# Four edits to the gated feed-forward stages of a two-layer encoder: other places for tiles, other queues for turns, fewer and later seven-product blocks, additions by DMA

## The chip, the cores and the metric

The kernel runs on one core of a Trainium2 chip, as one program. The metric is the device time in microseconds (us) of one execution; the time before is the median of three timed runs. The profile is that of one further execution, whose own time is given beside its span.

## The reference, cut to what matters

The program computes two layers of an encoder over 256 tokens of width 2048 in float32. Each layer is an attention mixer and then a gated feed-forward stage; only the second is touched.

```python
def conv_ffn(x, w_up, conv_w, conv_b, w_down):          # D_FF = 5632
    h = jnp.einsum("bsd,df->bsf", x, w_up)
    g, u = h[..., :D_FF], h[..., D_FF:]
    gp = jnp.pad(g, ((0, 0), (1, 1), (0, 0)))
    g = conv_w[0] * gp[:, :-2] + conv_w[1] * gp[:, 1:-1] + conv_w[2] * gp[:, 2:] + conv_b
    return jnp.einsum("bsf,fd->bsd", jax.nn.gelu(g) * u, w_down)

def reference(...):
    for layer in range(2):
        ...
        h = h + mix
        h = h + conv_ffn(rmsnorm(h, ln_ffn[layer]), ...)
    return rmsnorm(h, ln_final)
```

In the program `g` is the gate, `u` the factor.

## The kernel before

**Products.** Every float32 matrix is split in two parts that TensorE multiplies in its rounded float32 form: a high part (a cast on ScalarE, line 231) and the rest (a subtraction on VectorE, line 234). A product is then three matmuls, high by high, high by low and low by high (lines 195 to 197). Weights stream from HBM in units of 128 x 1024 values: a load on SyncE's queue into one of five `raw` places, the cast into one of four `wh`, the subtraction into one of four `wl`. A unit holds 256 input rows for 512 columns, and feeds twelve matmuls of 128 x 512 (two token halves, two blocks of 128 rows, three matmuls each).

**The feed-forward stage.** 5632 hidden values are 44 blocks of 128, taken four at a time: `up_group` j makes 512 columns of the gate (`x` = 0) and 512 of the factor (`x` = 1), each for both token halves, in four `gm` banks of PSUM, over eight units. Groups 0 to 5 are the first half, 6 to 10 the second (`HALVES`). After a half's groups its products go through the down projection: `chunk_pair` takes two output chunks of 512 columns at a time, chunks 0 and 1, then 2 and 3, over 12 units in the first half and 10 in the second, and `finish_chunk` adds each chunk's result to the residual `h` (line 376). The last pair of the program is handled by `finish_all`.

**Seven products.** Where two chunks share a unit, the eight block products of a 2 x 2 by 2 x 2 matrix product (24 matmuls) can be made with seven (21 matmuls). This is done for one unit of every `up_group` (`UPK`) and for some units of the down projection: for blocks 1 to 4 of the first half and 1 to 3 of the second, counted from the half's first (in the program's last pair for the first two of them). `column_forms` makes sums and differences of the weights on VectorE (lines 944 to 948) and splits them; `row_forms` does the same for the left operand; `seven_products` (lines 970 to 972) gathers in four extra PSUM banks, `b1`, `b5`, `b6`, `b7`, what belongs to several results. After the last seven-product unit of a pair, `extra_sums` adds them to `h` on VectorE (lines 978 to 989).

**From tokens to features.** At the end of a group each side is scaled from PSUM into a tile (line 877, two instructions, one for each token half), turned in blocks of 32 x 32 on VectorE (line 279) and put in its place by sixteen DMAs of 32 KB each (line 273), eight on SyncE's queue and eight on GpSimd's. Both sides use the same tile, `sc`, so the factor's first instruction waits until the gate's DMAs have read it. `convolved` (lines 893 to 898) then runs on the gate, and `multiplied` (line 921) makes the product, its forms where the block is a seven-product one, and its split parts `prod`.

**What sets the order.** The program is written in order with a small list of things to do later (`later`, `tick`). A scheduler then orders the instructions of each engine, but for those that `keep_in_program_order` pins. Each engine and each queue works strictly in its order. Tiles with one tag share a ring of places; the scheduler adds the waits.

## Time and profile before

| | |
|---|---|
| median of three runs | 2413.26 us (2413.17 to 2413.91) |
| profiled execution, its own time | 2413.16 us |
| its span (first to last instruction) | 2411.4 us |
| TensorE busy | 2392.2 us, 99% |
| VectorE busy | 1881.6 us, 78% |
| ScalarE busy | 1378.7 us, 57% |
| GpSimd busy | 436.4 us, 18% |
| HBM read | 458.48 MB, 191 GB/s over the span |
| feed-forward stages | about 661 to 1372 us and 1690 us to the end |

Matmuls overlap each other, so the mean duration of one (390 ns for 128 x 512) is longer than the time from one to the next, and a busy TensorE says that matmuls follow each other, not at which pace. Idle time of TensorE stands in the waits, with the instruction that ended it. A group's line gives its count, its busy time, the mean of one, and the idle time of its engine just before. "Landing" is the time from a DMA's issue until its data is there. The rows of lines, timelines and waits use the line numbers printed above.

### The profile page before, as it was taken

To read this page: it belongs to the slowest core of one execution; us is meant where nothing else is said; L and a number is where in the kernel's file an instruction comes from. 1 tells how busy PE (TensorE), PEld (TensorE's weight loads), DVE (VectorE), ACT (ScalarE), POOL (GpSimd) and SP (SyncE) were. 2 spreads that over 40 slices of the span, in tenths; PEclk is the share of its full clock that TensorE was granted. 3 is DMA by queue.
4 is the path that set the end of the run, shared out by engine and by line. 5 is a ranking of instruction groups with operands and counts; after the bars stand their busy time and mean duration, and the time that the engine had idled before them with its cause. 6 is when DMAs were issued, how large, how long until landed. Compare 5 with 4: busy or idle time off the path is not lost. (4 is left out here: it accounts for less than half of the span.)

```text
span 2411.4 us, 33193 instructions
## 1 busy us (share of the span) xinstructions
PE 2392.2 (99%) x10883; PEld 1977.5 (82%) x10883; DVE 1881.6 (78%) x2491; ACT 1378.7 (57%) x1960; POOL 436.4 (18%) x764
## 2 busy tenths in 40 slices
PE   9999999999999999999999999999999999999998
PEld 7888888888888888888788888888887888888787
DVE  6576567666778898878889867776788988789897
ACT  6455455566665565545656667555665655555554
POOL 1042033322211211002121200322112210022210
PEclk9999999999999999999999999999999999999999
DMA  8678678766767777667776754667677766677774
GB/s 305 205 196 239 197 195 240 216 201 185 219 193 228 212 221 206 208 204 212 218 213 213 241 185 139 189 198 211 188 228 218 219 197 208 215 213 220 226 214 152
DMA packets 329773, 505.66 MB, mean 210 GB/s; under 512 B 204152, under 2 KB 205560, under 8 KB 329600
## 3 DMA queue, kind: packets, MB, share of 16 engines
q1 hardware_dynamic: 304720, 475.92, 62.8%
q0 software_dynamic: 24448, 26.97, 7.1%
q8 instruction: 85, 1.39, 0.2%
q14 instruction: 88, 0.72, 0.1%
q10 hardware_dynamic: 432, 0.66, 0.1%
HBM read 458.48 MB, written 2.18 MB: 191 GB/s over the span
## 5 line engine op out<-in xcount | busy, mean ns | idle before, releaser
L231 ACT CAST wh<-raw 128x1024 fp32r<-128x1024 f32 (+1 forms) x897 | 931.9, 1048 | 799.4 <-PE gm L197 589.9
L234 DVE TENSOR_TENSOR wl<-raw,wh 128x1024 fp32r<-128x1024 f32 (+1 forms) x897 | 1081.4, 1216 | 380.1 <-ACT wh L231 363.6
L196 PE MATMUL gm<-wl,yT 128*128 128x512 f32 x2092 | 815.8, 390 | 3.1 <-DVE wl L234 2.9
L195 PE MATMUL gm<-wh,yT 128*128 128x512 f32 x2092 | 814.8, 391 | 2.8 <-DVE sc L877 2.8
L197 PE MATMUL gm<-wh,yT 128*128 128x512 f32 x2092 | 812.1, 390 | 0.1
L196 PEld LDWEIGHTS gm<-wl,yT 128*128 128x128 f32 x2092 | 392.8, 188 | 86.7 <-DVE wl L234 6.8
L195 PEld LDWEIGHTS gm<-wh,yT 128*128 128x128 f32 x2092 | 392.7, 188 | 85.6 <-DVE sc L877 4.0
L197 PEld LDWEIGHTS gm<-wh,yT 128*128 128x128 f32 x2092 | 392.7, 188 | 83.0 <-DVE yT L240 0.6
L273 POOL DMA_DIRECT2D qk<-sc x352 | 202.4, 583 | 1047.0 <-DVE sc L279 381.4
L196 PE MATMUL gm<-wl,prod 128*128 128x512 f32 x486 | 189.3, 389 | 0.0
L195 PE MATMUL gm<-wh,prod 128*128 128x512 f32 x486 | 188.7, 389 | 0.0
L197 PE MATMUL gm<-wh,prod 128*128 128x512 f32 x486 | 188.3, 389 | 0.0
L195 PEld LDWEIGHTS gm<-wh,prod 128*128 128x128 f32 x486 | 91.2, 188 | 19.5 <-DVE sc L877 0.4
L196 PEld LDWEIGHTS gm<-wl,prod 128*128 128x128 f32 x486 | 91.2, 188 | 19.2 <-DVE wl L234 0.3
L197 PEld LDWEIGHTS gm<-wh,prod 128*128 128x128 f32 x486 | 91.2, 188 | 19.0
L273 POOL DMA_DIRECT2D qk<-z x128 | 73.9, 585 | 172.5 <-DVE z L279 156.0
L196 PE MATMUL gm<-wl,mix 128*128 128x512 f32 x256 | 100.1, 391 | 0.8 <-DVE wl L234 0.8
L195 PE MATMUL gm<-wh,mix 128*128 128x512 f32 x256 | 100.0, 391 | 0.0
L197 PE MATMUL gm<-wh,mix 128*128 128x512 f32 x256 | 99.6, 390 | 0.0
L273 POOL DMA_DIRECT2D hT<-z x72 | 41.4, 583 | 194.4 <-PE gm L197 75.6
L856 ACT ACTIVATE sum<-sum,rstd 128x512 f32<-128x512 f32 x88 | 60.3, 719 | 12.9 <-DVE sum L847 12.9
L279 DVE STREAM_TRANSPOSE sc<-sc 128x1024 f32<-128x1024 f32 (+1 forms) x55 | 66.7, 1212 | 1.0
(355 smaller groups left out, 2716.0 us busy)
## 6 DMA issues: line engine op xcount, KB each, us to landing
raw<-in_up SPq DMA_DIRECT2D x352, 512.0 KB, 4.6
raw<-in_down SPq DMA_DIRECT2D x176, 512.0 KB, 4.4
raw<-in_eva_qk SPq DMA_DIRECT2D x96, 512.0 KB, 4.4
raw<-in_eva_v SPq DMA_DIRECT2D x46, 512.0 KB, 5.2
raw<-in_evb_qk SPq DMA_DIRECT2D x32, 512.0 KB, 4.8
raw<-in_ev_out SPq DMA_DIRECT2D x32, 512.0 KB, 4.3
raw<-in_od_qk SPq DMA_DIRECT2D x32, 512.0 KB, 4.1
raw<-in_od_out SPq DMA_DIRECT2D x32, 512.0 KB, 4.4
```

What stands on the lines that cost most here:

```text
L195: T.matmul(ps[t], ah, wh[:, sl], start=(kt == 0), stop=False)
L196: T.matmul(ps[t], ah, wl[:, sl], start=False, stop=False)
L197: T.matmul(ps[t], al, wh[:, sl], start=False, stop=(kt == nk - 1))
L231: first = S.copy(dst_h, src)
L234: V.tensor_tensor(dst_l, src, dst_h.bitcast(F32), op=ALU.subtract)
L273: (nc.sync if i % 2 else G).dma_start(dst[j * 32:(j + 1) * 32, :, i * 32:(i + 1) * 32], z[i * 32:(i + 1) * 32].rearrange("p (b j c) -> p b ...
L279: V.transpose(p, p)
L856: S.activation(sums[x][t], sums[x][t], AF.Copy, scale=rstd[0][:, t:t + 1])
```

## The change

- The factor's tile is `z` from another pool, and no longer the gate's `sc`. The second of the two scaling instructions is pinned to its place in the program.
- In these turns three of four source blocks are moved by GpSimd's queue: twelve DMAs there and four on SyncE's, instead of eight and eight. Other turns keep eight and eight.
- The first half has three seven-product blocks (1, 2, 3) instead of four. In each block it is the second of its two units and not the first: units 3, 5, 7 and not 2, 4, 6 (and 8).
- The forms of the left operand have other places, since `z` is taken: the first block's in `rw` and `bias`.
- `extra_sums` makes its two intermediate sums on VectorE and copies `b1` and `b5` on ScalarE; four DMAs of GpSimd that add to their destination, in order, bring them into `h`. In the second half the units that both chunks share before the last ones number 8 instead of 7.

```diff
-HALVES = ((0, 6, (1, 2, 3, 4)), (6, 11, (1, 2, 3)))
+HALVES = ((0, 6, (1, 2, 3)), (6, 11, (1, 2, 3)))
...
-    def moved(z, dst):
+    def moved(z, dst, on_sync=(1, 3)):
...
-                (nc.sync if i % 2 else G).dma_start(
+                (nc.sync if i in on_sync else G).dma_start(
...
-            z = new_sc().rearrange("p t (f k) -> p (t f) k", k=P)
+            z = (tmp.tile([P, 8, P], F32, name=nm("z"), tag="z", bufs=1) if x else
+                 new_sc().rearrange("p t (f k) -> p (t f) k", k=P))
             for t in range(2):
-                V.scalar_tensor_tensor(...)
+                out = V.scalar_tensor_tensor(...)
+                if t:
+                    tc.keep_in_program_order(out)
...
-            turned(z..., sides[x]...)
+            turned(z..., sides[x]..., (3,))
...
-        f = form_sums(*(c4[:, k, t * P:(t + 1) * P] for k in range(2) for t in range(2)))
+        f = form_sums(*(c4[:, 2 + k, t * P:(t + 1) * P] for k in range(2) for t in range(2)))
...
-            forms[2 * (j - g0)] = row_forms(c4, *new_forms(g0, seven.index(j - g0)))
+            forms[2 * (j - g0) + 1] = row_forms(c4, new_forms(g0, seven.index(j - g0)))
...
     def extra_sums(extra, c):
         b1, b5, b6, b7 = extra
-        s = tmp.tile([P, 512], F32, name=nm("sum"), tag="rx")
+        s, x0, s5, x1 = (tmp.tile([P, 512], F32, name=nm("sum"), tag=tag) for tag in ("rx", "ry", "ry", "rx"))
         S.copy(s, b1)
-        V.tensor_tensor(hchunk(0, c), hchunk(0, c), s, op=ALU.add)
-        V.tensor_tensor(s, s, b6, op=ALU.add)
-        V.tensor_tensor(hchunk(0, c + 1), hchunk(0, c + 1), s, op=ALU.add)
-        def rest():
...
-        later(1, rest)
+        S.copy(s5, b5)
+        V.tensor_tensor(x0, s, b6, op=ALU.add)
+        V.tensor_tensor(x1, x0, b7, op=ALU.add)
+        def added(dst, src):
+            tc.keep_in_program_order(G.dma_start(dst, src, accum_op=ALU.add))
+        def twice(x):
+            return x.unsqueeze(1).to_broadcast([P, 2, 512])
+        added(hchunk(0, c), s)
+        added(hchunk(0, c + 1), x0)
+        added(two(h[:, 1, c * 512:(c + 2) * 512]), twice(x1))
+        added(h[:, :, (c + 1) * 512:(c + 2) * 512], twice(s5))
...
-        pss = pair_head(src, c, act, forms, sorted(forms), nu - 3, nk)
+        heads = nu - 3 if nu > 10 else nu - 2
+        pss = pair_head(src, c, act, forms, sorted(forms), heads, nk)
```

How the instructions stand on the engines follows from the scheduler. First place: VectorE at the end of group 0, before the change (`gm` are the group's PSUM banks, `wl` the low parts of weight units, lines 894 and 896 the convolution):

```order
L234 TENSOR_TENSOR wl_6526<-raw_6523,wh_6525 128x1024
L877 SCALAR_TENSOR_TENSOR sc_6462<-gm_6081,rstd_6182,sum_6235 128x4x128
L894 SCALAR_TENSOR_TENSOR qk_6448<-qk_6358,convw,qk_6448 128x255 x2
L896 SCALAR_TENSOR_TENSOR qk_6448<-qk_6358,convw,qk_6448 128x255 x2
L894 SCALAR_TENSOR_TENSOR qk_6448<-qk_6358,convw,qk_6448 128x255 x2
L896 SCALAR_TENSOR_TENSOR qk_6448<-qk_6358,convw,qk_6448 128x255 x2
L877 SCALAR_TENSOR_TENSOR sc_6462<-gm_6082,rstd_6182,sum_6237 128x4x128
L234 TENSOR_TENSOR wl_6544<-raw_6541,wh_6543 128x1024
L279 STREAM_TRANSPOSE sc_6462<-sc_6462 128x1024
```

The same place on VectorE in the changed program (line 878 answers to 877, 897 and 899 to 894 and 896, 952 to 945):

```order
L878 SCALAR_TENSOR_TENSOR z_6462<-gm_6081,rstd_6182,sum_6235 128x4x128
L878 SCALAR_TENSOR_TENSOR z_6462<-gm_6082,rstd_6182,sum_6237 128x4x128
L234 TENSOR_TENSOR wl_6544<-raw_6541,wh_6543 128x1024
L279 STREAM_TRANSPOSE z_6462<-z_6462 128x1024
L952 TENSOR_TENSOR raw_6576<-raw_6577,raw_6576 128x512
L234 TENSOR_TENSOR wl_6584<-raw_6577,wh_6583 128x1024
L897 SCALAR_TENSOR_TENSOR qk_6448<-qk_6358,convw,qk_6448 128x255 x2
L899 SCALAR_TENSOR_TENSOR qk_6448<-qk_6358,convw,qk_6448 128x255 x2
```

The two scaling instructions now follow each other, and the convolution stands behind the turn and behind another weight unit. Second place: VectorE some fifteen instructions on, in group 1, before (line 921 multiplies gate and factor, lines 845 to 848 sum the extra banks of the group's seven-product unit):

```order
L234 TENSOR_TENSOR wl_6634<-raw_6631,wh_6633 128x1024
L921 TENSOR_TENSOR qk_6448<-qk_6448,qk_6465 128x1024
L845 TENSOR_TENSOR sum_6623<-sum_6622,tp_6574 128x512
L234 TENSOR_TENSOR prod_6560<-qk_6448,prod_6560 128x256
L234 TENSOR_TENSOR prod_6563<-qk_6448,prod_6563 128x256
L234 TENSOR_TENSOR prod_6566<-qk_6448,prod_6566 128x256
L234 TENSOR_TENSOR prod_6569<-qk_6448,prod_6569 128x256
L846 TENSOR_TENSOR sum_6624<-sum_6623,s_6575 128x512
L234 TENSOR_TENSOR wl_6652<-raw_6649,wh_6651 128x1024
```

The same place on VectorE in the changed program (line 928 answers to 921):

```order
L234 TENSOR_TENSOR wl_6634<-raw_6631,wh_6633 128x1024
L234 TENSOR_TENSOR wl_6652<-raw_6649,wh_6651 128x1024
L928 TENSOR_TENSOR qk_6448<-qk_6448,qk_6465 128x1024
L845 TENSOR_TENSOR sum_6623<-sum_6622,tp_6574 128x512
L234 TENSOR_TENSOR wl_6674<-raw_6671,wh_6673 128x1024
L234 TENSOR_TENSOR prod_6560<-qk_6448,prod_6560 128x256
L234 TENSOR_TENSOR prod_6563<-qk_6448,prod_6563 128x256
L234 TENSOR_TENSOR prod_6566<-qk_6448,prod_6566 128x256
L234 TENSOR_TENSOR prod_6569<-qk_6448,prod_6569 128x256
L846 TENSOR_TENSOR sum_6624<-sum_6623,s_6575 128x512
L234 TENSOR_TENSOR wl_6692<-raw_6689,wh_6691 128x1024
```

Two weight units that stood behind the run of other work, `wl_6652` and the one after it, now stand ahead of it and in its middle. Third place: VectorE in the second half's first pair of the first layer, in the changed program (lines 987 and 988 are the two sums that are left, line 376 adds a finished chunk to `h`; the first two are chunk 0, the last two chunk 1):

```order
L234 TENSOR_TENSOR wl_11802<-raw_11799,wh_11801 128x1024
L987 TENSOR_TENSOR sum_11726<-sum_11725,tp_11514 128x512
L988 TENSOR_TENSOR sum_11728<-sum_11726,s_11515 128x512
L234 TENSOR_TENSOR wl_11820<-raw_11817,wh_11819 128x1024
L234 TENSOR_TENSOR wl_11867<-raw_11864,wh_11866 128x1024
L376 TENSOR_TENSOR h<-h,gm_11387 128x512
L376 TENSOR_TENSOR h<-h,gm_11388 128x512
L308 STREAM_TRANSPOSE z_11780<-h 128x1024
L234 TENSOR_TENSOR wl_11885<-raw_11882,wh_11884 128x1024
L234 TENSOR_TENSOR wl_11903<-raw_11900,wh_11902 128x1024
L376 TENSOR_TENSOR h<-h,gm_11389 128x512
L376 TENSOR_TENSOR h<-h,gm_11390 128x512
```

Beside it GpSimd's queue at that place, with the semaphores that each DMA waits for (`DMASW` are those of GpSimd's DMAs; the third and fourth carry two chunks each):

```order
L991 DMA h<-sum_11725 128x512 [waits DMASW6_49,Activation_49]
L991 DMA h<-sum_11726 128x512 [waits DMASW7_49,DVE_49]
L991 DMA h<-sum_11728 128x2x512 [waits DMASW0_49,DVE_49]
L991 DMA h<-sum_11727 128x2x512 [waits DMASW1_49,DMASW7_49,DMASW0_49,Activation_49]
```

Before the change six additions on VectorE, lines 979 to 989, stood between the weight units here. Now two do, the fourth DMA waits for the second and the third, and each addition of line 376 stands behind the landing of a DMA: the second for the third DMA, the third for the second and the fourth.

More of the change, by code (lines that the diff above doesn't have):

```diff
@@ L267, in squares, with turned @@
                 tc.keep_in_program_order(ins)
-    def moved(z, dst):
+    def moved(z, dst, on_sync=(1, 3)):
         for i in range(4):
             for j in range(4):
-                (nc.sync if i % 2 else G).dma_start(
+                (nc.sync if i in on_sync else G).dma_start(
                     dst[j * 32:(j + 1) * 32, :, i * 32:(i + 1) * 32],
                     z[i * 32:(i + 1) * 32].rearrange("p (b j c) -> p b j c", j=4, c=32)[:, :, j, :])
-    def turned(p, dst):
+    def turned(p, dst, *on_sync):
         V.transpose(p, p)
-        moved(p, dst)
+        moved(p, dst, *on_sync)
     def y_tile(src, gain, kt, pin=False):
@@ L874, in up_group @@
                     tick()
-            z = new_sc().rearrange("p t (f k) -> p (t f) k", k=P)
+            z = (tmp.tile([P, 8, P], F32, name=nm("z"), tag="z", bufs=1) if x else
+                 new_sc().rearrange("p t (f k) -> p (t f) k", k=P))
             for t in range(2):
-                V.scalar_tensor_tensor(z.rearrange("p (f t) k -> p t f k", t=2)[:, t],
+                out = V.scalar_tensor_tensor(z.rearrange("p (f t) k -> p t f k", t=2)[:, t],
                                        pss[x][t].rearrange("p (f k) -> p f k", k=P), rstd[0][:, t:t + 1],
                                        sums[x][t].rearrange("p (f k) -> p f k", k=P), op0=ALU.mult, op1=ALU.add)
+                if t:
+                    tc.keep_in_program_order(out)
             sides[x] = quad(2 * x)
-            turned(z.rearrange("p b k -> p (b k)"), sides[x].rearrange("p f (t k) -> p (f t) k", k=P))
+            turned(z.rearrange("p b k -> p (b k)"), sides[x].rearrange("p f (t k) -> p (f t) k", k=P), (3,))
             if not x:
@@ L902, in new_forms, with row_forms @@
         if n == 0:
-            t = tmp.tile([P, 2, 4, P], F32R, name=nm("form"), tag="z", bufs=1)
-        elif g0:
+            high = tmp.tile([P, 4, P], F32R, name=nm("form"), tag="rw", bufs=1)
+            return [(high[:, 2 * x:2 * x + 2], att.tile([P, 2, P], F32R, name=nm("form"), tag="bias", bufs=2))
+                    for x in range(2)]
+        if g0:
             t = acts.tile([P, 2, 4, P], F32R, name=nm("form"), tag=f"act{18 + 2 * n}")
-        elif n < 3:
+        else:
             t = att.tile([P, 2, 4, P], F32R, name=nm("form"), tag="pt", bufs=2)
-        else:
-            return tuple(tmp.tile([P, 4, P], F32R, name=nm("form"), tag=tag, bufs=1) for tag in ("rw", "junk"))
-        return t[:, 0], t[:, 1]
-    def row_forms(c4, fh, fl):
-        f = form_sums(*(c4[:, k, t * P:(t + 1) * P] for k in range(2) for t in range(2)))
-        split(fh, fl, f)
-        return [(fh[:, x], fl[:, x]) for x in range(4)]
+        return [(t[:, 0], t[:, 1])]
+    def row_forms(c4, parts):
+        f = form_sums(*(c4[:, 2 + k, t * P:(t + 1) * P] for k in range(2) for t in range(2)))
+        form = []
+        for high, low in parts:
+            n = high.shape[1]
+            split(high, low, f[:, len(form):len(form) + n])
+            form += [(high[:, x], low[:, x]) for x in range(n)]
+        return form
     def multiplied(j, sides, prod, forms, g0, seven):
@@ L1016, in chunk_pair @@
         for x in range(2):
-            for u in range(nu - 3, nu):
+            for u in range(heads, nu):
                 a_unit(pss[x], src[c + x], u, act, nk)
@@ L1334, in _paired @@
         for c in (0, 2):
-            for u in (2 * (g0 + j) for j in seven):
-                spared = c and g1 == FT // 4 and u - 2 * g0 not in [2 * j for j in seven[:LAST]]
+            for u in (2 * (g0 + j) + 1 for j in seven):
+                spared = c and g1 == FT // 4 and u - 2 * g0 not in [2 * j + 1 for j in seven[:LAST]]
                 layers = slice(0, 1 if spared else 2)
```

6 lines of the change are left out of this document (removed).

## The prediction

> **What bounds the kernel now.** I read the page's shares first, then the granted clock, then one stretch without stalls, then TensorE's waits.
>
> ```profile
> PE 2392.2 (99%) x10883; PEld 1977.5 (82%) x10883; DVE 1881.6 (78%) x2491; ACT 1378.7 (57%) x1960; POOL 436.4 (18%) x764
> core 0: 2411.4 us, clock 0.999
> 2040.00:2100.00 60.00, 60.00 (x266) 49.57 (x265) 49.64 (x53) 30.46 (x34) 0.00 (x0) 1.00 0.65 212
> 700.00:900.00 200.00, 199.26 (x873) 162.78 (x872) 173.45 (x231) 120.63 (x155) 42.30 (x74) 1.00 0.75 220
> PE gm L196 <- DVE wl L234: 3.7, 5, 0.8
> PE gm L195 <- DVE sc L877: 2.8, 2, 1.5
> PE tp L970 <- ACT form L231: 2.0, 1, 2.0
> PE s L554 <- DVE warm L550: 1.2, 1, 1.2
> PE s L475 <- DVE sc L759: 0.7, 1, 0.7
> ```
>
> TensorE is busy 99% at a clock of 0.999. The stretch from 2040 to 2100 us holds feed-forward matmuls of 128 x 512 alone (the end of a down projection and the start of the next groups): 266 in 60.00 us, 0.226 us each. That pace is the floor, and only two things move the time: the number of matmuls, and TensorE's idle time. The waits give little of the latter: 3.7 + 2.8 + 2.0 us in three rows that touch the feed-forward stages, each longest wait 2.0 us or less; the others are 1.2 us and less and lie elsewhere. VectorE is the next engine: 173.45 of 200 us in the first layer's groups, so it can be late there for a moment, but it has slack in the other stretch (49.64 of 60 us). So whatever VectorE is spared there is worth nothing by itself, and the most that all edits together can win is some 8 us of waits, plus what stretches matmuls without a row of its own (below).
>
> **The change part by part.**
>
> *Fewer seven-product blocks.* A seven-product unit is 21 matmuls, a plain one for the same two chunks 24. The first half loses one block in two pairs in two layers: 4 units, 12 matmuls more, 12 x 0.226 = **+2.7 us**. Nothing hides that, TensorE being the floor. Weights read and loads issued stay the same. What VectorE is spared in each (lines 944 to 948 once, 0.67 to 0.69 us each, and some 1.5 subtractions of 1.2 us, 4.5 us in all) lies under TensorE, and so does the shift from a block's first unit to its second: it gives the forms one unit more time, at a place where no row of waits stands.
>
> *The factor's own place, and the pin.* The second row of waits is TensorE held by line 877. Its two cases are at 1184 and 1827 us, in the third group of the first layer's second half and of the second layer's first half. VectorE around the first:
>
> ```profile
> 1179.44 0.75 DVE L877 SCALAR_TENSOR_TENSOR sc<-gm,rstd,sum 128x512 f32<-128x512 f32 x1 [1.86 <-DMA qk<-sc]
> 1180.10 0.87 DVE L894 SCALAR_TENSOR_TENSOR qk<-qk,convw,qk 128x255 f32<-128x255 f32 x2
> 1180.89 0.88 DVE L896 SCALAR_TENSOR_TENSOR qk<-qk,convw,qk 128x255 f32<-128x255 f32 x2
> ...
> 1183.26 0.75 DVE L877 SCALAR_TENSOR_TENSOR sc<-gm,rstd,sum 128x512 f32<-128x512 f32 x1
> ```
>
> The first of the two waited for the gate's DMAs to leave `sc`, then eight convolution instructions (3.2 us) ran before the second, which frees the bank that TensorE needs for the next group. Both causes go: the tile is another, and by the order of the program the two follow each other. **-2.8 us.** What is late next is the convolution, which now stands behind the turn and a weight unit, and with it line 928; I look at that next.
>
> *Turns mostly on GpSimd.* One turn's issues before, at the end of the last layer's fourth group of the second half, and what came behind them:
>
> ```profile
> 2258.69 5.87 SPq L273 DMA_DIRECT2D qk<-sc  x8
> 2259.42 4.64 POOL L273 DMA_DIRECT2D qk<-sc  x8 [0.37 <-DVE t L944]
> 2264.67 9.56 SPq L128 DMA_DIRECT2D raw<-in_up  x6
> 2271.57 1.05 ACT L231 CAST wh<-raw 128x1024 fp32r<-128x1024 f32 x1 [4.44 <-DMA raw<-in_up]
> 2274.26 0.61 ACT L231 CAST form<-t 128x512 fp32r<-128x512 f32 x1
> qk<-sc SPq DMA_DIRECT2D x352, 32.0 KB, 2.4
> qk<-sc POOLq DMA_DIRECT2D x352, 32.0 KB, 2.3
> ```
>
> An issue takes 5.87/8 = 0.73 us on SyncE and 4.64/8 = 0.58 us on GpSimd. Eight and eight end after 5.9 us; twelve on GpSimd take 7.0 us, four on SyncE 2.9 us. The data lands as fast from either queue, so a turn is complete about 1.1 us later. That is covered for the factor: since its scaling ends 3.2 us sooner, its turn still starts earlier than before. For the gate, which starts at the same time, the convolution is 1.1 us later, and by the new order it stands one weight unit later in any case. GpSimd has room: 42.30 of 200 us. The 2.9 us that SyncE gains matter where a weight load stands behind a turn. Here the load left at 2264.67, the moment SyncE was through, ScalarE idled 4.44 us for it, and the cast of `form` behind it held TensorE for the 2.0 us of the third row. With SyncE free 2.9 us sooner the load can leave sooner, if its place is free by then, which no row says. Between 0 and -2.0 I take half: **-1.0 us.**
>
> *VectorE's order in the groups after the first of a half.* Four of the five waits of the first row are at 725, 1111, 1754 and 2142 us (the fifth is in an attention projection, at 1607). VectorE before the first:
>
> ```profile
> 718.68 1.22 DVE L234 TENSOR_TENSOR wl<-raw,wh 128x1024 fp32r<-128x1024 f32 x1
> 719.81 1.22 DVE L921 TENSOR_TENSOR qk<-qk,qk 128x1024 f32<-128x1024 f32 x1
> ...
> 723.48 1.22 DVE L234 TENSOR_TENSOR wl<-raw,wh 128x1024 fp32r<-128x1024 f32 x1
> ```
>
> From one weight unit's end to the next's 4.8 us pass, while TensorE uses one in 12 x 0.226 = 2.7 us. In the new order two units stand ahead of that run and in its middle, the longest gap is about 2.0 + 1.2 us, and the wait should shrink. The work is no less, though, and line 928 must not come late. The four are worth 4 x 0.74 = 3.0 us; between 0 and -3.0 I take two thirds, since the order removes the run itself: **-2.0 us.**
>
> *Additions by DMA.* For each of the eight pairs VectorE loses lines 979 to 989 and keeps two sums:
>
> ```profile
> L986 DVE TENSOR_TENSOR h<-h,sum 128x1024 f32<-128x1024 f32 x8 | 9.8, 1222 | 0.2
> L989 DVE TENSOR_TENSOR h<-h,tp 128x1024 f32<-128x1024 f32 x8 | 9.7, 1214 | 0.0
> L981 DVE TENSOR_TENSOR h<-h,sum 128x512 f32<-128x512 f32 x8 | 5.5, 689 | 0.2
> L980 DVE TENSOR_TENSOR sum<-sum,tp 128x512 f32<-128x512 f32 x8 | 5.4, 680 | 0.0
> ```
>
> Six instructions, 1.22 + 1.21 + 4 x 0.68 = 5.2 us, become two of 0.68; 3.8 us a pair, under TensorE. What is new is a wait: line 376 stands on VectorE behind the landings. Count from T, the end of the last seven-product unit. The two sums, 0.68 each behind the last matmul's end, are ready at T + 1.8; after an issue of 0.6 the third DMA is on its way at T + 2.4 and lands L later; the fourth waits for it and lands at T + 3.0 + 2L. In the second half TensorE ends chunk 0 at T + 6.1 (27 matmuls by the order) and has weights for three more units, until T + 14.3. Behind line 376 VectorE has a turn (1.24) and the next unit's subtraction (1.22): the third DMA may land until T + 11.1, which is L = 8.7. For chunk 1 two more units are ready, until T + 19.7; the fourth may land until T + 17.2, which is L = 7.1. So nothing is lost up to L = 7.1 us, and 2L - 14.2 us a pair beyond it. That counts for three pairs: both of the first layer's second half and the first of the last layer's. In the first half chunk 0 ends 63 matmuls (14.2 us) after T and chunk 1 99 (22.3 us), enough even at L = 9.3. The trace has no adding DMA; the nearest rows:
>
> ```profile
> raw<-in_down SPq DMA_DIRECT2D x176, 512.0 KB, 4.4
> out<-h SPq DMA_DIRECT2D x6, 256.0 KB, 2.4
> h<-in_x SPq DMA_DIRECT2D x4, 512.0 KB, 9.3
> lnf<-in_lnf POOLq DMA_DIRECT2D x4, 256.0 KB, 4.6
> ```
>
> The same 512 KB, plain and beside this traffic, land in 4.4 us; rows of 2 KB into the same `h`, in the crowded first microseconds, in 9.3. An addition also has to fetch what stands at its destination, and the DMA engines are 0.65 busy in such a stretch, so I place it between, at 7.2 to 7.3, just past the point: 0.3 us in each of three pairs, **+1.0 us**, between 0 (below L = 7.1) and 3 x 4.4 = +13.2 (L = 9.3). The program's last pair has four units between T and chunk 2, and VectorE is not full there: nothing.
>
> The Trainium skill (DMA: Bandwidth & Descriptors, "Anatomy of one DMA") fits a GpSimd DMA as about 2.0 us plus bytes over 436 GB/s, an estimate of 3.2 us for 512 KB; by it the term would be 0, but the plain 256 KB of `lnf` above took 4.6 us, so the rows stand.
>
> *The sum.* The profiled execution took 2413.16 us (its span 2411.4 and 1.8 around it), 0.1 below the median of 2413.26. 2413.2 + 2.7 - 2.8 - 1.0 - 2.0 + 1.0 = **2411.1 us**.
>
> **The rivals.**
>
> *The additions land late (slower).* If the second operand doubles the time, L = 2 x 4.4 = 8.8 us: 2 x 8.8 - 14.2 = 3.4 us a pair, 10.2 in three; 2411.1 - 1.0 + 10.2 = 2420.3; at L = 9.3 it is 2423.3. It costs from L = 7.1, eats up what is won at 7.6 (3 x 1.0 us) and decides from 8.5 (3 x 2.8 = 8.4 us). For it: every row with 2 KB rows or from GpSimd is above 4.4. Against it: VectorE may be further ahead than the order makes it, and `out<-h`, which reads the same memory, took 2.4. The Trainium skill (Collectives: The Full Stack, "The bandwidth ceiling") says that an addition in a DMA emits two reads for one write and runs at half a copy's rate; no run here shows it yet.
>
> *The waits move instead of going.* VectorE's work in the groups is the same, so a unit may be late at the next step, behind the later line 928 or the convolution. For it: 173.45 busy of 200. Against it: the order has no run as long. Then only the matmuls and the DMA term count, the gains being taken back: 2413.2 + 2.7 + 1.0 = 2416.9.
>
> *All small waits go.* Matmuls that use the forms are stretched beyond the 390 ns of the others:
>
> ```profile
> L196 PE MATMUL gm<-wl,yT 128*128 128x512 f32 x2092 | 815.8, 390 | 3.1 <-DVE wl L234 2.9
> L971 PE MATMUL tp<-form,form 128*128 128x512 f32 x37 | 15.9, 431 | 0.0
> L970 PE MATMUL tp<-form,form 128*128 128x512 f32 x37 | 15.4, 417 | 2.0 <-ACT form L231 2.0
> ```
>
> That is 37 x (41 + 27) ns = 2.5 us. With loads and forms earlier all of it and all three rows could go: 2413.2 + 2.7 - 2.8 - 3.0 - 2.0 - 2.5 = 2405.6. Against it: the forms' casts still wait behind the same work on ScalarE.
>
> **How the numbers follow.** About 0.2% (4.8 us) can be told from no change, so faster is below 2408.4 and slower above 2418.1. My forecast (2408.5 to 2414.5) has 0.45, the late additions 0.20, the moved waits 0.18, the full gain 0.17. The late additions fall above 2418.1 but for a little that others give back (slower 0.19); forecast and moved waits lie inside, with a rest of the full gain (same 0.65); faster 0.16. The range goes from the full gain, 2405.5, to the late additions at L = 9.3, 2423.3, and leaves some 0.15 outside.
>
> **What would show it.** The matmul count rises by 12. TensorE's wait for the scaling (line 878) is gone; if it stays, the pin or the place did not do it. The waits for `wl` at the second group of each half shrink or move. A turn shows twelve GpSimd issues of about 0.58 us, over 7 us, and the load behind it leaves sooner. The DMAs of line 991 show L: up to 7 us with no VectorE wait that reaches TensorE, or 8 and more with TensorE idle at the ends of the second half's pairs, waiting for `wl` behind line 376. The prediction is wrong if these rows hold and the time still moves elsewhere, or if an adding DMA is so slow (over 10 us) that the first half's additions wait too.

## The result, and the profile after

The changed kernel takes 2440.35 us (median of 4 runs, 2439.62 to 2446.86), the kernel before 2413.55 on the same chip: a ratio of 1.0112, 95% interval 1.0100 to 1.0125, some 27 us slower. The prediction was 2411.1 us. The profiled execution took 2440.24 us with a span of 2438.5.

First what the prediction named. The page of the changed kernel (busy time, share of the span, number of instructions):

```profile
span 2438.5 us, 33053 instructions
PE 2405.4 (99%) x10895; PEld 1987.1 (81%) x10895; DVE 1829.6 (75%) x2429; ACT 1372.3 (56%) x1962; POOL 575.3 (24%) x972
```

TensorE has the 12 matmuls more, and VectorE has 52 us of work less. So neither engine's amount of work tells of 27 us; the "99%" hides it, since a matmul that runs at half pace counts as busy too. TensorE's waits of the changed kernel (engine and line, what it waited for, us in total, times, the longest) tell more. Rows of a run carry the line numbers of that run's own kernel: line 978 here is line 971 of the kernel before, a matmul of a seven-product unit.

```profile
PE gm L195 <- DVE h L376: 14.0, 6, 3.2
PE gm L195 <- ACT yT L237: 4.2, 1, 4.2
PE gm L196 <- DVE wl L234: 2.1, 9, 0.7
PE gm L978 <- DVE wl L234: 1.5, 2, 0.8
```

The first row is new. The tile in it is `gm`, a PSUM bank: TensorE does not wait for weights, as I had assumed, but for line 376 to add a finished chunk to `h` and so free its bank. The second row follows from it: the next mixer's first tiles are made of that `h`. The scaling's row (line 877, 2.8 us) is gone. The wait for the form (2.0 us) is gone too. The waits for `wl` are as long as before in sum, 2.1 + 1.5 us against 3.7, though at other places.

What holds line 376 is seen on VectorE. The timeline of the changed kernel at the end of the first pair of layer 0's second half (start, duration, instruction, and in brackets the idle time before it and what ended it):

```profile
1309.87 0.68 DVE L987 TENSOR_TENSOR sum<-sum,tp 128x512 f32<-128x512 f32 x1
1310.58 0.69 DVE L988 TENSOR_TENSOR sum<-sum,s 128x512 f32<-128x512 f32 x1
...
1315.96 0.69 DVE L376 TENSOR_TENSOR h<-h,gm 128x512 f32<-128x512 f32 x1 [1.33 <-DMA h<-sum]
1323.57 0.69 DVE L376 TENSOR_TENSOR h<-h,gm 128x512 f32<-128x512 f32 x1 [6.92 <-DMA h<-sum]
...
1329.53 1.29 DVE L376 TENSOR_TENSOR h<-h,gm 128x512 f32<-128x512 f32 x2 [1.74 <-issue]
```

GpSimd in the same stretch, the four additions of that pair (the two in the middle share a row):

```profile
1308.04 0.93 POOL L991 DMA_DIRECT2D h<-sum  x1 [30.31 <-ACT sum L985]
1310.85 2.08 POOL L991 DMA_DIRECT2D h<-sum  x2 [1.87 <-DVE sum L987]
1324.01 1.19 POOL L991 DMA_DIRECT2D h<-sum  x1 [11.09 <-DMA h<-sum]
```

The third addition goes out at 1311.6 (by its own record in the trace) and lands just before 1323.5: 11.9 us. The fourth is behind it, goes out at 1324.0 and lands before 1329.5: 5.4 us. The list of transfers, which has the median of both kinds together, shows neither:

```profile
h<-sum POOLq DMA_DIRECT2D x16, 512.0 KB, 8.1
h<-sum POOLq DMA_DIRECT2D x16, 256.0 KB, 7.8
qk<-sc POOLq DMA_DIRECT2D x264, 32.0 KB, 5.5
```

Over all eight pairs the third took 11.3 to 13.1 us (7.5 in the program's last pair), the fourth 5.0 to 8.6. TensorE at that place:

```profile
1320.74 0.39 PE L197 MATMUL gm<-wh,prod 128*128 128x512 f32 x1
1324.32 0.79 PE L195 MATMUL gm<-wh,prod 128*128 128x512 f32 x1 [3.19 <-DVE h L376]
1324.91 0.63 PE L196 MATMUL gm<-wl,prod 128*128 128x512 f32 x1
...
1327.61 0.40 PE L197 MATMUL gm<-wh,prod 128*128 128x512 f32 x1
1330.36 0.49 PE L195 MATMUL gm<-wh,prod 128*128 128x512 f32 x1 [2.36 <-DVE h L376]
```

A chunk has two banks, one for each token half. The pair ends at 1320.3; the next pair's first three matmuls go into the bank that line 376 had freed at 1316.7. The fourth waits for the first chunk's other bank, and nine matmuls later TensorE waits for the second chunk's. Behind each stop the matmuls follow each other every 0.43 us, not 0.23. The two stops and what follows each, as four stretches (length, busy time of PE, PEld, DVE, ACT and POOL with their instructions, granted clock, DMA share, GB/s):

```profile
1320.97:1324.32 3.35, 0.16 (x2) 0.00 (x1) 0.71 (x2) 0.00 (x0) 0.31 (x1) 0.93 0.33 72
1324.32:1327.74 3.42, 3.42 (x9) 2.63 (x9) 3.42 (x3) 2.62 (x4) 2.78 (x5) 0.57 0.64 111
1327.84:1330.36 2.52, 0.16 (x1) 0.03 (x1) 0.83 (x2) 0.06 (x1) 2.52 (x5) 1.00 1.00 129
1330.70:1334.10 3.40, 3.40 (x10) 2.63 (x9) 2.47 (x3) 1.98 (x5) 0.00 (x0) 0.50 0.60 93
```

The granted clock falls to a half for a few microseconds behind a stop. By the spacing of the matmuls (less the usual 0.23 us) the stops come in twos at 1324 and 1330 (3.35 and 2.53 us), 1385 and 1402 (2.72 and 4.37) and 2372 and 2379 (3.15 and 2.75), 18.9 us in three pairs, and 1.3 and 0.7 us at the ends of the two first halves (1053 and 2101 us).

### The profile page after: what moved, and what is told of

Its sections match the earlier page's. It is cut to its first block, busy times and chain, and to the rows that moved or that the text cites. A ratio compares the mean times of both kernels' runs of the same rounds, so it can differ in the third digit from the quotient of the medians.

```text
span 2438.5 us, 33053 instructions
## 1 busy us (share of the span) xinstructions
PE 2405.4 (99%) x10895; PEld 1987.1 (81%) x10895; DVE 1829.6 (75%) x2429; ACT 1372.3 (56%) x1962; POOL 575.3 (24%) x972
## 3 DMA queue, kind: packets, MB, share of 16 engines
q8 instruction: 85, 1.39, 0.2%
## 4 chain that ended last, share of the span: by engine, by line
PE 76%; DVE 7%; DMA 6%; issue 6%; POOL 2%; ACT 2%; SPq 1%; DVEq 0%; POOLq 0%; ACTq 0%
PE gm L196 21%; PE gm L195 21%; PE gm L197 21%; DVE wl L234 3%; DMA h<-sum 2%; PE gm L145 2%; DMA raw<-in_up 2%; ACT wh L231 1%; DMA qk<-sc 1%; PE gm L150 1%; POOL qk L273 1%; SPq L273 1%; DVE qk L897 1%; DVE qk L899 1%; PE tp L977 1%
## 5 line engine op out<-in xcount | busy, mean ns | idle before, releaser
L273 POOL DMA_DIRECT2D qk<-sc x264 | 152.5, 586 | 611.6 <-issue 409.5
L273 POOL DMA_DIRECT2D qk<-z x392 | 226.4, 585 | 290.6 <-DVE z L279 252.0
L195 PE MATMUL gm<-wh,prod 128*128 128x512 f32 x518 | 204.5, 395 | 10.9 <-DVE h L376 10.9
L197 PE MATMUL gm<-wh,prod 128*128 128x512 f32 x518 | 203.9, 394 | 0.0
L196 PE MATMUL gm<-wl,prod 128*128 128x512 f32 x518 | 203.9, 394 | 0.0
L195 PEld LDWEIGHTS gm<-wh,prod 128*128 128x128 f32 x518 | 98.8, 191 | 33.6 <-DVE h L376 7.0
L991 POOL DMA_DIRECT2D h<-sum x32 | 33.5, 1076 | 376.1 <-ACT sum L985 273.5
L196 PEld LDWEIGHTS gm<-wl,prod 128*128 128x128 f32 x518 | 98.8, 191 | 20.5
L197 PEld LDWEIGHTS gm<-wh,prod 128*128 128x128 f32 x518 | 98.6, 190 | 20.7
L951 DVE TENSOR_TENSOR t<-raw 128x512 f32<-128x512 f32 x45 | 31.1, 690 | 45.2 <-DMA raw<-in_up 35.2
```

The lines of the kernel that those rows point to most:

```text
L195: T.matmul(ps[t], ah, wh[:, sl], start=(kt == 0), stop=False)
L196: T.matmul(ps[t], ah, wl[:, sl], start=False, stop=False)
L197: T.matmul(ps[t], al, wh[:, sl], start=False, stop=(kt == nk - 1))
L273: (nc.sync if i in on_sync else G).dma_start(dst[j * 32:(j + 1) * 32, :, i * 32:(i + 1) * 32], z[i * 32:(i + 1) * 32].rearrange("p (b j c) ...
L951: V.tensor_tensor(t1, w12, w11, op=ALU.subtract)
L991: tc.keep_in_program_order(G.dma_start(dst, src, accum_op=ALU.add))
```

## The experiments

All ratios are to the kernel before on the same chip, with 95% intervals.

### The additions against the rest of the change

Two runs take the change apart at its largest new piece: all but the additions, and the additions alone.

```diff
 # sums_on_vector: in the changed kernel
-        added(hchunk(0, c), s)
-        added(hchunk(0, c + 1), x0)
-        added(two(h[:, 1, c * 512:(c + 2) * 512]), twice(x1))
-        added(h[:, :, (c + 1) * 512:(c + 2) * 512], twice(s5))
+        V.tensor_tensor(hchunk(0, c), hchunk(0, c), s, op=ALU.add)
+        V.tensor_tensor(s, s, b6, op=ALU.add)
+        V.tensor_tensor(hchunk(0, c + 1), hchunk(0, c + 1), s, op=ALU.add)
...
```

The second run, `dma_sums_alone`, is the reverse edit in the kernel before.

> The changed kernel with the six VectorE instructions of the old extra sums in place of the four adding DMAs; places, pin, turns and the three later blocks stay. Theory A (the additions by DMA are late for line 376, so PSUM banks come free late, and TensorE's granted clock halves after each such stop): the four terms of my sum that do not concern the DMAs should be left, 2413.2 + 2.7 - 2.8 - 1.0 - 2.0 = 2410.1, between 2407 and 2415; no granted clock of 0.5 between 1300 and 1410 us. Rival B (the turns on GpSimd or the later blocks make the loss): still above 2425.

> The kernel before, with the additions by DMA as its only change. Theory A: before, the last seven-product unit of a second-half pair is followed by three units a chunk (2 x 36 matmuls, 16.3 us) and not two (2 x 24, 10.9 us). The third DMA lands some 14 us after that unit, so TensorE finds the first chunk's banks free; the fourth lands at about 20 us, some 2 us late. So a smaller loss than in the changed kernel: 2415 to 2425. Rival B: no loss here (2413 or less). Rival C (the additions cost the same wherever they stand, by the traffic they make): about 2413 + 27 = 2440.

Without the additions by DMA: 2411.57 us, ratio 0.9995 (0.9986 to 1.0005); between 1300 and 1410 us no row of a halved clock. With the rest of the change in place, the whole loss is the additions': 28 us by the two ratios. In the profiles the two differ by 25.0 us (spans 2438.5 and 2413.5): 17.4 in gaps between matmuls that are over 260 ns longer than usual, and 7.5 in gaps that are 20 to 260 ns longer, most of them at the halved clock.

The additions alone: 2465.63 us, 1.0214 (1.0199 to 1.0229), 53 us. I expected a smaller loss than in the change and found one twice as large. At the end of the first pair of layer 0's second half the theory held (0.7 us at 1341), not at the end of its second pair (4.2 us at 1414) nor of the last layer's first (4.3 us at 2405), and in the first halves, where I expected nothing, TensorE stopped 5.8 to 5.9 us at 997, 1068 and 2058 and 3.8 at 2126. VectorE in that run at the first of them:

```profile
986.75 0.69 DVE L376 TENSOR_TENSOR h<-h,gm 128x512 f32<-128x512 f32 x1 [6.96 <-DMA h<-sum]
987.35 1.22 DVE L234 TENSOR_TENSOR wl<-raw,wh 128x1024 fp32r<-128x1024 f32 x1
988.49 0.68 DVE L944 TENSOR_TENSOR t<-raw 128x512 f32<-128x512 f32 x1
...
994.61 0.69 DVE L945 TENSOR_TENSOR raw<-raw,raw 128x512 f32<-128x512 f32 x1 [3.70 <-DMA raw<-in_down]
995.22 1.22 DVE L234 TENSOR_TENSOR wl<-raw,wh 128x1024 fp32r<-128x1024 f32 x1
996.35 1.27 DVE L376 TENSOR_TENSOR h<-h,gm 128x512 f32<-128x512 f32 x2
```

While line 376 holds VectorE for 7 us, no weights are split and no places for loads come free, so the load of the next pair's first seven-product block is late; its line 945 then waits 3.70 us for that load, and it stands ahead of line 376 of the second chunk. In the changed kernel that block is one unit later. Two more runs, further down, put this to the test.

### Why the additions land late

```diff
 # plain_copies: in the changed kernel
-            tc.keep_in_program_order(G.dma_start(dst, src, accum_op=ALU.add))
+            tc.keep_in_program_order(G.dma_start(dst, src))
 # four_small_adds: in the changed kernel, four sums instead of two, one addition a tile
-        S.copy(s5, b5)
...
+        V.tensor_tensor(x0, x0, b5, op=ALU.add)
+        V.tensor_tensor(y0, x1, b5, op=ALU.add)
...
         added(hchunk(0, c), s)
+        added(hchunk(1, c), x1)
         added(hchunk(0, c + 1), x0)
-        added(two(h[:, 1, c * 512:(c + 2) * 512]), twice(x1))
-        added(h[:, :, (c + 1) * 512:(c + 2) * 512], twice(s5))
+        added(hchunk(1, c + 1), y0)
```

> The changed kernel with the same four DMAs a pair as plain copies: the additions are left out, the extra sums overwrite h. Tells the adding from the queueing. Theory A1 (the third DMA is late because every 2 KB packet that adds takes 176 ns on an engine that the loads keep full, against 85 to 92 ns for plain ones): it lands some 3 us sooner, 9 us after its issue, TensorE's stops in the second half are 1 us or none, 2413 to 2422. Theory A2 (it is late because it stands behind two others in GpSimd's queue and the start of that queue takes 4 us, whatever the packets do): third DMA at 11 us and more, 2432 to 2441.

> The changed kernel with four additions of 256 KB a pair, one for each tile of a chunk, the first chunk's two first (VectorE makes four sums of 0.68 us instead of two); no DMA waits for another. Theory A: the first chunk's additions end where the second DMA ends now, 4.9 us sooner, the second chunk's 5 to 6 us sooner: the stops of 2.5 to 3.4 us go, and the halved clock with them: 2410 to 2416. If each issue and each queue place cost a fixed time and not the bytes: 2425 or more.

Plain copies, which leave the adding out: 2419.02 us, 1.0021 (1.0012 to 1.0030). The third of a pair lands in 6.5 to 7.8 us (5.7 in the last pair), the fourth of the second halves in 3.1 to 3.3, and line 376 waits 3.74 us where it waited 6.92. The page's list for that run:

```profile
h<-sum POOLq DMA_DIRECT2D x16, 512.0 KB, 6.7
h<-sum POOLq DMA_DIRECT2D x16, 256.0 KB, 5.3
```

By the packet records of the two traces, an addition moves 2 KB in 176 ns of an engine's time, the same transfer without it 4 KB in 159: 2.2 times the time a byte. The Trainium skill (Collectives: The Full Stack, "The bandwidth ceiling") puts the adding step of a reduce-scatter at half a copy's rate, since an addition reads two operands for one write. The 2.2 times of these traces come near that. The engines are shared: from 1315 to 1321 us of the changed kernel they carried some 50 packets of additions and some 50 of weight loads in each microsecond, about 16 x 1 us of engine time, so all 16 were full. When VectorE stops and the loads dry up, the fourth addition moves 90 packets a microsecond and lands in 5.4 us.

Four small additions: 2417.29 us, 1.0017 (1.0007 to 1.0026), just above the 2410 to 2416 expected. The result is the same, and the bytes are 1.0 MB a pair instead of 1.5, of which 0.5 MB and not 1.0 stand ahead of the first chunk's line 376. At the pair shown above the last landing that the first chunk needs comes 10.2 us after the first issue, and the second chunk's after 13.4, where the changed kernel had 15.4 and 21.4. So the loss came from how the additions were cut and chained: the bytes in the queue ahead of the one that is waited for, at the adding rate, and, for the second chunk, an addition that went out only when the third had landed. This run changes both and does not part them. Both runs stay some 5 to 6 us above `sums_on_vector` (0.9995), and what that rest is stays open.

### Whether the deadline is the bank

```diff
 # two_blocks_late_half: in the changed kernel
-HALVES = ((0, 6, (1, 2, 3)), (6, 11, (1, 2, 3)))
+HALVES = ((0, 6, (1, 2, 3)), (6, 11, (1, 2)))
```

> The changed kernel without the last seven-product block of each second half, so that the extra sums start two units (5.4 us of TensorE) sooner before the chunks end; the DMAs stay as they are. Theory A (banks are freed by line 376 after the third and fourth landing, about 14 and 20 us after the last block): the stops in the second halves go, except perhaps 0 to 2 us at the second landing; 9 matmuls more cost 2.0 us: 2414 to 2422. If the additions cost by their traffic or by VectorE held in line 376: 2435 and more.

2415.11 us, 1.0002 (0.9993 to 1.0011), with 9 matmuls more than the changed kernel and every addition still there. Its row of TensorE's waits behind line 376:

```profile
PE gm L195 <- DVE h L376: 2.7, 2, 2.1
```

Two units of lead time remove 11.3 of the 14.0 us and all windows of halved clock but for the program's end, though the additions land no sooner: at the same pair 15.6 and 23.6 us after the first issue. Additions that lie early enough cost nothing that these runs can tell: 1.0002 here against 0.9995 without them, of which the 9 matmuls are 0.0008. So neither their traffic nor the hold on VectorE makes the loss by itself; that the banks and not the weights are the deadline is read from TensorE's waits above.

### Whether the halved clock costs time

```diff
 # filled_gaps: in the changed kernel, behind a pair (n = 11) and between two chunks (n = 9)
+        for i in range(n):
+            tc.keep_in_program_order(T.matmul(ps, act[0][:, 0, 0:P], y, start=i == 0, stop=i == n - 1))
```

> The changed kernel with 51 matmuls more that nobody reads (11 behind each second-half pair that stops, 9 between the first and the second chunk of the next one's first unit: 2.5 and 2.0 us), in the gaps of 2.5 to 3.4 us in which TensorE stands still for banks. If the halved granted clock behind each gap costs time, it should be faster by 3 to 6 us (1.4 to 1.7 us for each of the windows of 3.41 us that end in no other wait): 2434 to 2437, with no clock of 0.5 there. If the clock is not set by the gap, or costs nothing: the same time, 2440, or up to 2 us more.

2444.94 us, 1.0126 (1.0109 to 1.0143): not faster, and by the intervals not different from the changed kernel. Half of the expectation held: the windows of 0.5 at 1324, 1331 and 1385 us are gone, of the 10.24 us from 2371.7 on 3.41 are left, and only the one at 1402, behind a gap that I did not fill, is longer (6.83). So the stops do set the clock. But the time did not come back. The stretches behind the second stop, first in this run (where TensorE goes on at 1328.5), then in the changed kernel (at 1330.4; columns as above):

```profile
1340.00:1344.00 4.00, 3.24 (x14) 2.45 (x15) 2.98 (x4) 2.08 (x5) 0.54 (x1) 1.00 0.93 233
1344.00:1352.00 8.00, 5.80 (x23) 3.86 (x22) 7.76 (x12) 6.51 (x8) 0.00 (x0) 1.00 0.67 236
```

```profile
1340.00:1344.00 4.00, 4.00 (x19) 3.34 (x18) 4.00 (x6) 1.06 (x1) 1.61 (x3) 1.00 0.84 131
1344.00:1352.00 8.00, 8.00 (x37) 6.60 (x36) 6.77 (x11) 5.63 (x9) 0.00 (x0) 1.00 0.96 349
```

At full clock TensorE reached the next units before their weights were there and stood still for them, at 1341, 1347 and 1352 us for 1.0 to 1.2 us each. In the changed kernel it has no such wait. The slow matmuls lay over a supply of weights that was late anyway, with VectorE held in line 376, so the 7.5 us of slow matmuls can't be put down to the clock alone: without it, time was lost to the weights.

### The other parts, one at a time

```diff
 # places_alone: the kernel before with the factor's own tile and the pin
+            z = (tmp.tile([P, 8, P], F32, name=nm("z"), tag="z", bufs=1) if x else
+                 new_sc().rearrange("p t (f k) -> p (t f) k", k=P))
...
+                if t:
+                    tc.keep_in_program_order(out)
...
+            return [tuple(att.tile([P, k, P], F32R, name=nm("form"), tag=tag, bufs=2) for _ in range(2))
+                    for k, tag in ((3, "bias"), (1, "bias2"))]
 # turns_alone: the kernel before
-                (nc.sync if i % 2 else G).dma_start(
+                (nc.sync if i in on_sync else G).dma_start(
...
 # blocks_alone: the kernel before
-HALVES = ((0, 6, (1, 2, 3, 4)), (6, 11, (1, 2, 3)))
+HALVES = ((0, 6, (1, 2, 3)), (6, 11, (1, 2, 3)))
...
-            forms[2 * (j - g0)] = row_forms(c4, *new_forms(g0, seven.index(j - g0)))
+            forms[2 * (j - g0) + 1] = row_forms(c4, *new_forms(g0, seven.index(j - g0)))
...
-        pss = pair_head(src, c, act, forms, sorted(forms), nu - 3, nk)
+        heads = nu - 3 if nu > 10 else nu - 2
+        pss = pair_head(src, c, act, forms, sorted(forms), heads, nk)
```

In `turns_alone` the turns of gate and factor pass (3,), as in the change: three of four source blocks go by GpSimd's queue; `turns_and_places` is both of the first two edits.

> The kernel before with the factor's own tile and the pin alone (the first form's products move to the places of two bias tiles, as four blocks are kept; turns, blocks and sums as before). My terms: -2.8 us for TensorE's wait on line 877, and whatever of the -2.0 at the second groups comes from VectorE's order: 0.9980 to 0.9990 of the time before, no wait of TensorE on the scaling. Rival (the waits move): the row of line 877 goes but wl rows grow by as much, 0.9995 to 1.0005.

> The kernel before with twelve of a turn's sixteen transfers on GpSimd as its only change. My term: -1.0 us, between 0 and -2.0, 0.9992 to 1.0000: the load behind a turn leaves earlier and the wait for a form is shorter. Rival (the gate's turned tile lands later, as 5.5 us and not 2.3 stands in the changed kernel's list of transfers, and the convolution with it): 1.0005 and more.

> The kernel before with three blocks a half, on the second unit of each group, and one unit more ahead of the chunks in the second half; sums on VectorE, places and turns as before. My term: 12 matmuls more, +2.7 us, nothing else, 1.0011. Rival (VectorE, spared some 4.5 us in each of four pairs and with the forms due later, gives it back): 1.0000 and less. Second rival (the later last block leaves line 376 and the sums less time before the banks are needed, also without DMAs): 1.002 and more.

> The kernel before with the turns on GpSimd and the factor's own tile and pin (four blocks on the first units, sums on VectorE). Theory D: the 98 us that the turns cost alone came from the factor's scaling, and TensorE behind it, waiting for the gate's slow turn to leave the shared tile, and from all that follows late; with a tile of its own most goes: 2410 to 2435 (the forms are made of the turned tiles and needed on the first units, so some waits for forms may stay). Rival: the late turned tiles themselves cost (forms, convolution): above 2460.

Places alone: 2418.32 us, 1.0017 (1.0008 to 1.0027). The row of the scaling is gone, but the time is 4 us longer, not 2.8 shorter; TensorE waits 4.1 us for `wl` and 2.6 for forms. With four blocks the first form had to go to other tiles than in the change, in two pieces, so a part of this may be that run's own.

Turns alone: 2510.75 us, 1.0408 (1.0391 to 1.0424). 98 us, the largest number of this study, for an edit priced at -1.0. TensorE's first rows in that run, two of VectorE's, and one turn on SyncE and GpSimd:

```profile
PE gm L195 <- DVE sc L877: 28.9, 20, 3.0
PE tp L970 <- ACT form L231: 19.9, 12, 4.0
```

```profile
DVE sc L877 <- DMA qk<-sc: 20.3, 16, 3.0
DVE qk L921 <- DMA qk<-sc: 17.5, 14, 2.1
```

```profile
715.56 2.57 SPq L273 DMA_DIRECT2D qk<-sc  x4
718.22 16.71 SPq L128 DMA_DIRECT2D raw<-in_up  x9
```

```profile
715.82 6.91 POOL L273 DMA_DIRECT2D qk<-sc  x12 [12.30 <-DVE sc L279]
```

SyncE is through with its four after 2.6 us and issues weight loads from then on. GpSimd's transfers from the sixth on now meet them on the DMA engines: they land 4.4 to 6.4 us after their issue, and the turn that began at 715.6 is complete at 728.1, 12.6 us later. Before, with SyncE busy issuing its half of the turn for as long as GpSimd, no load came in between, and a turn at this place was complete 7.0 us after its begin. Where gate and factor share `sc`, the factor's scaling waits for that turn, TensorE for the scaling, and products and forms come late behind it.

Turns and places together: 2414.06 us, 0.9995 (0.9986 to 1.0004). The factor's own tile takes the 98 us away again, and no row of TensorE's waits is above 2.2 us in total. So the two parts are not terms of a sum: one is the condition of the other.

Blocks alone: 2418.05 us, 1.0016 (1.0007 to 1.0025), 3.9 us where 2.7 were expected; the interval holds 1.0011.

### Why the additions cost more alone, and whether the turns share in the loss

`dma_sums_later_blocks` is `blocks_alone` with the changed kernel's function for the extra sums. `dma_sums_half_turns` is the changed kernel with one edit:

```diff
-            turned(z.rearrange("p b k -> p (b k)"), sides[x].rearrange("p f (t k) -> p (f t) k", k=P), (3,))
+            turned(z.rearrange("p b k -> p (b k)"), sides[x].rearrange("p f (t k) -> p (f t) k", k=P))
```

> The kernel before with the additions by DMA and the three later blocks (turns and places as before). The additions alone cost 2.14%, more than the whole change (1.12%). Theory E (in that run the next pair's first seven-product block starts with the third unit, and on VectorE its line 945, which waits for a load that line 376 held up, stands ahead of line 376 of the second chunk, so the second bank came 3 to 4 us later still in the first halves; with the block one unit later that order is gone): 1.010 to 1.015. If the additions alone cost what they do for another reason: 1.02 and more.

> The changed kernel with the turns divided by halves again, everything else as changed, the additions by DMA too. If the loss is the additions' alone: 1.010 to 1.013 as in the changed kernel (1.0112). If the turns on GpSimd (same queue as the additions, and 5.5 us to land) add to it: 1.008 and less.

With the three later blocks the additions cost what they cost in the change: 2440.46 us, 1.0107 (1.0091 to 1.0122), and at the place of the first stop of 5.9 us VectorE runs line 376 ahead of the block's sums:

```profile
988.21 1.28 DVE L376 TENSOR_TENSOR h<-h,gm 128x512 f32<-128x512 f32 x2 [0.55 <-DMA h<-sum]
991.54 0.69 DVE L944 TENSOR_TENSOR t<-raw 128x512 f32<-128x512 f32 x1 [2.04 <-DMA raw<-in_down]
```

So the edit of the blocks, whose shift I costed at nothing, is worth some 26 us to the additions (1.0214 against 1.0107), where without them it cost 3.9. With the turns by halves the changed kernel takes 2442.33 us, 1.0120 (1.0106 to 1.0133): the turns have no part in the loss that this run can show.

### A version without the additions

```diff
 # four_blocks_vector: sums_on_vector with the fourth block of the first half back
-HALVES = ((0, 6, (1, 2, 3)), (6, 11, (1, 2, 3)))
+HALVES = ((0, 6, (1, 2, 3, 4)), (6, 11, (1, 2, 3)))
-        heads = nu - 3 if nu > 10 else nu - 2
+        heads = nu - 2
```

The first form stands in the bias tiles, as in `places_alone`, and the fourth in the tiles `rw` and `junk`, as in the kernel before. `half_turns_four` is the same kernel with the turns by halves, `three_blocks_half_turns` is `sums_on_vector` with the turns by halves.

> The changed kernel with the sums on VectorE and the fourth block of the first half back (12 matmuls fewer, its forms in the bias tiles). If the terms add: 2413.2 - 2.8 - 1.0 - 2.0 = 2407.4, 0.9976 of the time before, and 2.7 us less than the run with three blocks. If the fourth block costs VectorE what its matmuls save: no difference from that run (0.9995).

> The run with four blocks and the sums on VectorE, with the turns divided by halves again (eight of sixteen transfers on SyncE). My prediction gave the other division -1.0 us. Theory D (a turn on GpSimd is complete 5.6 us later, since SyncE issues weight loads meanwhile and the turn's 128-byte rows share the engines with them; the factor's own tile covers that): within 3 us of that run, that is 0.9975 to 0.9995 of the time before, so the division is worth nothing either way once the tile is there. If the earlier loads are worth what I took: 1 us or more slower than that run. If the late turns still cost something there: faster than that run, 0.9975 and less.

> The changed kernel with the sums on VectorE and the turns by halves: three blocks, places, pin. Beside the run with four blocks and turns by halves (0.9971) it prices the fourth block once more: 12 matmuls, 2.7 us, so 0.9982 if my term of +2.7 holds, 0.9971 and less if VectorE gives it back; and beside the run with the turns on GpSimd (0.9995) the division of the turns: equal within 0.1% if it is worth nothing.

| run | blocks in the first half | turns | median us | ratio |
|---|---|---|---|---|
| sums_on_vector | 3 | GpSimd | 2411.57 | 0.9995 (0.9986 to 1.0005) |
| three_blocks_half_turns | 3 | halves | 2415.80 | 1.0010 (1.0001 to 1.0018) |
| four_blocks_vector | 4 | GpSimd | 2409.71 | 0.9981 (0.9972 to 0.9990) |
| half_turns_four | 4 | halves | 2408.30 | 0.9971 (0.9960 to 0.9983) |

The last two beat both kernels; the best is 7 us faster than the kernel before on its chip, and 1.4% faster than the changed one by the two ratios. The division of the turns goes one way with three blocks (0.15%) and the other with four (0.10%), each within or at the edge of the intervals: I take it as worth nothing that these runs can show. The fourth block is worth 0.14% with one division (3.4 us, the 2.7 of the matmuls) and 0.39% with the other; why the second is larger is open.

## Why the prediction was wrong

**What bounds the kernel** was right: TensorE's matmuls and its idle time set the end, and the 27 us are idle time and slow matmuls.

**Additions by DMA, +1.0: the step that failed.** They cost some 28 us (0.9995 without them, 1.0112 with them), and the step was wrong in two places.

The first is the landing. I took L = 7.2 for the third and the fourth alike, from single transfers. Measured: 11.9 and 5.4 us at the place shown. The third stood behind 512 KB of other additions in the same queue, all at 2.2 times a copy's time per byte and beside weight loads; the fourth stood alone. The upper bound of 9.3 was a bound for one transfer and not for three in a row, so the range was too narrow as well. The condition at the end of the prediction ("over 10 us") is what happened.

The second is the deadline. Count from T = 1308.7, 27 matmuls before the first chunk's end, as the prediction did. The second sum ended at T + 2.6 and not at T + 1.8, since VectorE was still at a weight unit. The third addition landed at T + 14.8; I had allowed T + 11.1, which was about right (by the trace, T + 11.4). The fourth landed at T + 20.7; I had allowed T + 17.2, because TensorE had weights for two units more, and by that deadline this landing would have cost 3.5 us. But the pair ahead holds all four `gm` banks: TensorE ends it at T + 11.6, has twelve matmuls to do in the first chunk's banks and so needs the second's at T + 14.3. Line 376 and the hand-over take the last 0.9 us (1329.45 to 1330.36), so the fourth had to land by T + 13.4. It was 7.3 us late; the two stops and the slow matmuls between them add up to 3.35 + 2.53 + 1.5 = 7.4. With the right deadline even my own L, a landing at T + 17.4, would have given 4.0 us in such a pair, an estimate of 12 in three.

Three pairs were named as those that would lose, and three lost: 18.9 us of stops, with 2.0 more at the ends of the first halves, which I had called safe up to L = 9.3.

**The rival "the additions land late"** had the landing right, with a price of 10 to 13 us instead of 28, and the same wrong deadline. Its sentence that every row with 2 KB rows is above 4.4 us does not hold for `out<-h`, which moves 2 KB packets and took 2.4.

**Factor's place and pin, -2.8.** The row went as forecast. Alone the edit was worth nothing or less (1.0017): the rival "the waits move" describes it. Its real worth lies with the turns.

**Turns, -1.0.** The failing sentence is "the data lands as fast from either queue, so a turn is complete about 1.1 us later". The landing time belongs to what else is on the engines: 2.3 us before and 5.5 now, and in the run with the turns alone the turn shown was complete 5.6 us later (12.6 against 7.0). The freed SyncE did what I expected, and the wait for the form went; but the loads that it issues are what slows the turn.

**VectorE's order, -2.0.** The four waits at 725, 1111, 1754 and 2142 us are gone, and others of 0.9 to 1.0 us stand at 761 and 850, in the seven-product units of the up projections. In sum the rows have 3.6 us against 3.7: they moved.

**Blocks, +2.7.** Right (3.9, with 2.7 in the interval). That the shift of the blocks costs nothing holds, within the interval, without additions by DMA; with them the blocks' edit is worth 26 us.

**The four terms but the additions** add up to -3.1; measured -1.1, with an interval from -3.4 to +1.2. The sum holds within it, but its parts do not: places and turns together measured 0.9995 (0.9986 to 1.0004), where their terms and that of the order give 0.9976. So the agreement of the sum is in part luck.

## What to carry to other kernels

A transfer that something waits for is priced by all that stands ahead of it in its queue and by what else the engines carry at that time, not by the median landing of a single one. The deadline is the first resource that the waiting instruction frees: here four PSUM banks and not the weights. And parts of a change that share a tile or an order on one engine aren't terms of a sum: alone, these parts cost 0.17, 4.08, 0.16 and 2.14%, together 1.12%.

## What was not expected of the hardware

The granted clock falls to 0.5 behind short stops of TensorE, in windows of 3.41, 6.83 or 10.24 us. It did so behind the stops of 2.5 us and more in the changed kernel, and once behind one of 2.05 us, with the sums on VectorE (columns as above):

```profile
2316.00:2319.00 3.00, 1.12 (x5) 0.64 (x4) 3.00 (x7) 3.00 (x7) 0.00 (x0) 0.99 0.22 87
2319.00:2322.40 3.40, 3.40 (x9) 2.61 (x9) 3.40 (x5) 3.37 (x6) 0.00 (x0) 0.50 0.60 208
2322.40:2326.00 3.60, 3.60 (x17) 2.98 (x17) 3.56 (x5) 1.75 (x3) 0.00 (x0) 1.00 0.82 271
```

The kernel before had a stop of 2.1 us, ending at 2275, without it. The Trainium skill (TensorE: Matmul & The Clock Gate, "Part 1: The HAM clock gate") has windows of 3413 ns that do not start with the work, and half clock after at least one idle window. The length of the windows agrees; a stop need not fill one, as 2.05 us show.

What parts those two stops is how they lie to the windows. The falls of the clock within one trace lie whole multiples of 3.413 us apart. Cut at these points, the stop of 2.05 us lies in one window; the one of 2.1 us lies in two, with 0.6 us in the first and 1.5 in the second. In the 17 traces from 600 us on, leaving out the programs' ends and counting as idle what matmul starts over 0.45 us apart exceed 0.226 us by, all 34 windows at full clock with 2.06 us idle or more were followed by half clock, none with less than 1.92, and six of the eight in between.

An addition's issue on GpSimd takes 0.85 to 0.95 us for 256 KB and 1.18 to 1.39 for 512, where the plain copies took 0.55 to 0.58 and 0.71 to 0.73. The first addition of a pair sees its first packet 2.9 to 5.0 us after the issue begins, the fourth, alone and with few loads about, mostly 1.8; the first plain copy of a pair mostly 1.7 to 2.3. Why the first addition waits so long no run here shows.
